# HGRN values of seven heads through memory and VectorE transposes, the residual moved to later jobs, decode rows transposed in one batch, the second group's gate sums later

## The chip, the cores and the metric

The kernel runs on one core of a Trainium2 chip, in one launch. The core has a matrix engine (TensorE, PE in the profile), a vector engine (VectorE, DVE), an activation engine (ScalarE, ACT), a general engine (GpSimd, POOL), and a queue from which DMAs are issued in order (SyncE, SP). Each engine works through its own instructions in order and waits on the others by semaphores. The metric is device time in microseconds (us); the median of three runs before the change is 1764.88 us (1764.72 to 1768.95).

## The reference

One inference step of one decoder layer, in fp32, for a prompt of 1024 tokens and 8 decode rows, 1032 columns in all, with a model width of 1024:

```python
h = rmsnorm(x, w['norm1_w'])
proj = h @ w['w_in']
q_r, f_r, i_r, g_r, z, xbc_r, dt_r = jnp.split(proj, splits, axis=-1)
# group A: HGRN2, 8 heads of 128
f = lb + (1.0 - lb) * jax.nn.sigmoid(f_r)
log_f, k, q = jnp.log(f), 1.0 - f, jax.nn.silu(q_r)
o_a, S_h_new = hgrn2_mix(heads(q), heads(k), heads(i_r), heads(log_f), S_h)
o_a = rmsnorm(o_a, w['hgrn_norm_w']) * jax.nn.silu(heads(g_r))
# group B: Mamba-2, 16 heads of 64 in 2 groups
...
y = y.reshape(Bsz, L, D_SSM) * jax.nn.silu(z)
y = rmsnorm(y.reshape(Bsz, L, SSM_GROUPS, -1), w['ssm_norm_w'].reshape(SSM_GROUPS, -1))
x = x + jnp.concatenate([o_a, y], axis=-1) @ w['w_out']
h = rmsnorm(x, w['norm2_w'])
gate, val = jnp.split(h @ w['w_up'], 2, axis=-1)
gate, buf_f_new = causal_dwconv(gate, buf_f, w['ffn_conv_w'], w['ffn_conv_b'])
x = x + (jax.nn.silu(gate) * val) @ w['w_down']
```

In HGRN2 a head has queries q, keys k, values v (`i_r`) and a forget factor f per key channel. Within a chunk the output is a causal product of q and k with the decays between them, times v; between chunks a state of 128 x 128 is carried. The decode rows each have their own state, which is multiplied by f, gets k times v added, and is read by q. Outputs are the final rows and all new states.

## The kernel before, in words

Tensors stand with channels on the 128 partitions and tokens along the free axis. A product of fp32 precision is made of three passes in a shorter format, high x high, high x low, low x high; every weight tile is therefore loaded (`ws`, line 189), cast by ScalarE to its high half (`wh`, line 190), and VectorE makes the low half (`wl`, line 192). These tiles have two buffers each, and a weight load is issued two jobs ahead. `fetch` (lines 172 to 175) issues other loads on SP, in order behind the last weight load.

PE's order is written out by hand; that of the other engines comes from a planner. The input projection is a list of jobs of 72 matmuls (three chunks of 344 columns, 24 each). For each HGRN head h there are four jobs, f, q, v and sg. `drive` takes a stream of other PE work, cuts it into pieces with weights (the numbers that the stream yields), and places job matmuls between them. While head h is in work, the jobs of head h+1 run; under the last head, head 7, the first jobs of the output projection run. `after(n, work)` runs `work` when n more job matmuls have passed, `spread` runs a row of pieces n matmuls apart.

`head(h, t)`, from line 830, is one such stream. In order: the 8 decode values are transposed (line 834) and eight PE transposes of 128 x 128 turn the head's values v (channels x tokens) into `vt` (tokens x channels) in two PSUM banks, `vtp` (line 839), which ScalarE copies out (line 840). VectorE copies the decode values (line 842), they go to memory (843) and come back spread over the partitions (`vb`). GpSimd multiplies them by k (line 852) and adds them to the states `Sh` (854), which SP stores (855). Then the causal product within a chunk is built in levels: `near` computes small blocks on PE (names `a0` to `a6` in the profile, tile `a`), and between the levels `scale(lv)` multiplies q and k by running products of f: two VectorE products (lines 872 and 873), and, at every other level, two ScalarE copies (875 and 876). The tiles f, k, v and q themselves are the working space: after line 901, which writes q times f into the place of v, they hold scaled keys and queries by turns. `level` picks blocks into `amc` (line 897). At the end come the decode outputs (`od`, copied at line 943), the transposed keys (`ktp`, line 950), the products of keys with values (`kv`, 962 and 964) and the outputs (`o`, 987), where `vt` is first used. `hr_d` and `mix_d` carry the head's result through memory to the output projection.

The gate of the Mamba-2 part (`ssm_gate`, for g of 0 and 1) sums squares over four jobs of z; after the last, for each of three chunks, `rstd` makes a product with ones (`ms`) and three VectorE products (lines 649 to 651), 36 + 14 g matmuls after that chunk's end. After the third chunk `tail` makes four VectorE products of 128 x 1032 (line 694) with four stores. For g = 1 this falls into head 0.

The output projection is a list of jobs (r0.m: four rows of 128 input channels, two blocks of 128 outputs). Jobs 8.0, 8.2, 12.0, 12.2 come first, then 8.4, 8.6, 12.4, 12.6, then those of rows 0 and 4. Their inputs come from memory as `ml`, and are cast to `mh` by ScalarE (line 1023) and split by VectorE (1024). Jobs with r0 = 8 copy PSUM to `x` by ScalarE (line 1064), the others add by VectorE (1066). There are three PSUM banks for these products. The residual is x itself in channel order. At an earlier time 32 DMAs (`token_blocks`, 770 to 776) write x_prompt to memory in blocks of 32 x 32; for each output block, two loads of 128 x 512 (`xs`), two VectorE transposes of 32 x 32 blocks (line 793), and adds on GpSimd (line 790) put it onto `x`. The decode rows are loaded as 8 x 128 (`xd`), transposed on PE (`xtd`, line 797), and added by VectorE (798). This is spread into the jobs with r0 = 8.

Of the kernel before, what the change touches and what calls it, by code (L numbers as in the profile page):

```python
# [16 lines left out]
P = 128  # L17
DM = 1024
T = 1024
# [31 lines left out]
def hybrid_layer(  # L51
# [177 lines left out]
    def after(n, work):  # L229

        later.append([n, work])
# [421 lines left out]
    def ssm_gate(g):  # L653
        acc = []

        def z_job(i):
            j = g * 4 + i

            def begin():
                if i == 0:  # L660
                    acc.append(tl("g", "gacc"))
                if g:
                    ssm_decode(1, i)
                elif i < 2:
                    ssm_decode(0, i + 2)

            def evict(c, cs, ps):
                Y = Xg[g][i][:, cs]
                sz = tl("z", "sz")[:, :CH]
                A.activation(sz, ps, AF.Silu)  # L670
                V.tensor_tensor(Y, Y, sz, op=ALU.mult)
                if i == 0:
                    A.activation(acc[0][:, cs], Y, AF.Square)
                else:
                    A.activation(sz, Y, AF.Square)
                    (V if g or i == 3 else G).tensor_tensor(acc[0][:, cs], acc[0][:, cs], sz, op=ALU.add)
                if i == 3:
                    after(36 + 14 * g, lambda: rstd(c))
            in_job(f"z{j}", OFF_Z + j * P, evict, begin=begin)

        def rstd(c):
            cs = chunks[c]
            ps = bank("ms", "nx")
            mm(ps[:, :CH], ones, acc[0][:, cs])
            rstd_of(acc[0][:, cs], tl("z", "nt")[:, :CH], ps[:, :CH], 512)

            if c == NCH - 1:
                tail()

        def tail():  # L690
            for i in range(4):
                j = g * 4 + i
                Y = Xg[g][i][:, :NT]
                V.scalar_tensor_tensor(Y, Y, col("sn", j), acc[0][:, :NT], op0=ALU.mult, op1=ALU.mult)
                SP.dma_start(mix_d[8 + j], Y)

        for i in range(4):
            z_job(i)
# [29 lines left out]
    def once(work):  # L728
        def run():
# [19 lines left out]
    G.affine_select(eye8, eye8, pattern=[[1, ND], [-1, ND]], compare_op=ALU.is_equal, fill=0.0, base=0,  # L749
                    channel_multiplier=0)  # L750
    vd_d = dram.tile([H, ND, P], F32, name="vd_d")
    hr_d = dram.tile([H, 4, 256], F32, name="hr_d")

    am = const.tile([P, NC, P], F32, name="am")
# [12 lines left out]

    xb_d = dram.tile([KT, P, T], F32, name="xb_d")

    def token_blocks():  # L770
        for m in range(KT):
            for a in range(4):
                f0 = m * P + 32 * a
                SP.dma_start(xb_d[m, 32 * a:32 * a + 32].rearrange("j (b i) -> j b i", i=32),
                             x_prompt[0, :, f0:f0 + 32].rearrange("(b j) i -> j b i", j=32))
                yield

    def residual_load(m):
        ms = slice(m * P, (m + 1) * P)
        xs = [tl("d", "xs")[:, :512] for _ in range(2)]  # L780
        xd = small.tile([ND, P], F32, tag="xd", name=nm("xd"))
        for i in range(2):
            fetch(xs[i], xb_d[m][:, i * 512:(i + 1) * 512])
        fetch(xd, x_sample[:, 0, ms])
        return xs, xd

    def residual(out, xs, xd):

        def add(x_, y_):
            G.tensor_tensor(x_, x_, y_, op=ALU.add)  # L790

        for i0 in range(2):
            V.transpose(xs[i0], xs[i0])
            if i0 == 0:
                add(out[0][:, 0:512], xs[0])
                ps = bank("xtd", "nx")
                PE.transpose(ps[:, :ND], xd, ident[:ND, :ND])
                V.tensor_tensor(out[1][:, 508:516], out[1][:, 508:516], ps[:, :ND], op=ALU.add)
            else:
                add(out[0][:, 512:516], xs[1][:, 0:4])  # L800
                add(out[1][:, 0:508], xs[1][:, 4:512])
            yield
# [3 lines left out]
    def head_in(h):  # L806
        t = {}

        def f_end():
            f, k = t["f"], tl("big", "k")  # L810
            A.activation(f[:, :NT], f[:, :NT], AF.Identity, bias=lbt[:, 0, h:h + 1], scale=lbt[:, 1, h:h + 1])
            V.tensor_scalar(k[:, :NT], f[:, :NT], -1.0, 1.0, op0=ALU.mult, op1=ALU.add)
            t["k"] = k

        for n, off, func in (("f", OFF_F, AF.Sigmoid), ("q", OFF_Q, AF.Silu), ("v", OFF_I, AF.Copy),
                             ("sg", OFF_G, AF.Silu)):
            def evict(c, cs, ps, n=n, func=func):
                A.activation(t[n][:, cs], ps, func)

            def begin(n=n):  # L820
                t[n] = tl("e" if h == 0 and n == "f" else "big", n)

            if h == H - 1 and n == "sg":
                in_job_last(f"{n}{h}", off + h * P, evict, begin)
            else:
                in_job(f"{n}{h}", off + h * P, evict, begin, f_end if n == "f" else None)
        return t

    def head(h, t):
        f, k, q, v, sg = (t[n] for n in ("f", "k", "q", "v", "sg"))  # L830


        dps = bank("vd", "nx")
        PE.transpose(dps[:ND, :P], v[:, T:NT], ident)
        vt = [half("vt"), half("vt")]
        for hf in range(2):
            ps = bank("vtp")
            for i in range(4):
                PE.transpose(ps[:, blk[i]], v[:, hf * 512 + i * P:hf * 512 + (i + 1) * P], ident)
            A.copy(vt[hf], ps)  # L840
# [5 lines left out]
        for b0 in (0, 4):  # L846
            bs = slice(b0, b0 + 4)
            ds = slice(T + b0, T + b0 + 4)
            Sd, vb = tl("ld", "Sh"), tl("d", "vb")[:, :512]
            fetch(d4(Sd), state_hgrn[0, bs, h].rearrange("b k v -> k b v"))  # L850
            fetch(vb, vd_d[h, bs].rearrange("b n -> (b n)").unsqueeze(0).to_broadcast([P, 512]))
            G.tensor_tensor(d4(vb), d4(vb), cb(k[:, ds]), op=ALU.mult)
            V.tensor_tensor(d4(Sd), d4(Sd), cb(f[:, ds]), op=ALU.mult)
            G.tensor_tensor(Sd, Sd, vb, op=ALU.add)
            SP.dma_start(hgrn_sample[0, bs, h].rearrange("b k v -> k b v"), d4(Sd))
            Sds.append(d4(Sd))

# [81 lines left out]
            mm(ops[32 * g:32 * g + 32, :P], qb[:, b, :], Sds[b // 4][:, b % 4, :], start=(b < 4), stop=(b >= 4))  # L941
        odr = small.tile([P, P], F32, tag="odr", bufs=1, name=nm("odr"))
        V.tensor_copy(odr, ops[:, :P])
        yield 3.5

        for hf in range(2):
# [93 lines left out]
    def out_job(r0, m, halves=(0, 1), last=False):  # L1040
        def load():
            w = wload(w_out[0, r0 * P:(r0 + 4) * P, m * P:(m + 2) * P], 4, 2 * P,
                      kept=(r0 // 4 * 4 + m // 2, halves[0]) if len(halves) == 1 else None)
            return w, [residual_load(m + i) for i in range(2)] if r0 == 8 else None

        def run(loads):
            w, res = loads
            if r0 not in mixes:
                mixes[r0] = mix_load(r0)
            hi, lo = mixes[r0]  # L1050
            if res:
                for hf in range(2):
                    xpair[hf][m // 2] = tl("big", "x1")[:, :NT].rearrange("p (i t) -> p i t", i=2)
                    for i in range(2):
                        xh[hf][m + i] = xpair[hf][m // 2][:, i, :]
            for i in range(2):
                for hf in halves:
                    for c in range(2):
                        cs, ts_ = slice(c * QW, (c + 1) * QW), slice((2 * hf + c) * QW, (2 * hf + c + 1) * QW)
                        ps = psmm.tile([P, 512], F32, tag="mm", name=nm("mm"))[:, :QW]  # L1060
                        yield from steps(w, i * P, (i + 1) * P, hi, lo, ts_, ps)
                        x_ = xh[hf][m + i][:, cs]
                        if res:
                            A.copy(x_, ps)  # L1064
                        else:
                            V.tensor_tensor(x_, x_, ps, op=ALU.add)
                        if last:
                            final(m + i, x_, ts_)
                            if hf and c:
                                after(28, lambda m=m + i: weigh(m))  # L1070
                        yield True
                if res:
                    spread(residual([xh[hf][m + i] for hf in range(2)], *res[i]), 8)
        job(f"o{r0}.{m}" + (f".{halves[0]}" if len(halves) == 1 else ""), load, run)

    def final(m, x_, ts_):
# [27 lines left out]
    heads[0] = head_in(0)  # L1104
    ssm_gate(1)
    heads[1] = head_in(1)
    job("conv", None, once(lambda: spread(conv_states(), 60, lambda: spread(token_blocks(), 40))))
    for h in range(2, H):
        heads[h] = head_in(h)

# [395 lines left out]
```

## Time and profile before

| what | value |
|---|---|
| median of 3 runs | 1764.88 us |
| profiled execution | 1763.89 us |
| its span | 1762.2 us, mean TensorE clock 0.994 |
| PE busy | 1713.2 us, 97% |
| VectorE, ScalarE, GpSimd busy | 63%, 46%, 27% |
| head 0 | 380 to 443 us: PE busy 58.3 of 63 |
| head 4 | 631 to 694 us: PE busy 63.0 of 63 |
| head 7 and the output jobs after it | 819 to 930 us: PE busy 101.2 of 111 |
| values: PE transposes `vtp` | 64 x 272 ns; ScalarE copies 16 x 590 ns |
| residual: VectorE transposes `xs` | 16 x 696 ns |

The span runs from the first to the last instruction of the profiled execution; the time of that execution is 1.7 us longer, by what lies around the span. Busy time of PE is modelled from starts and includes overlap, so an entry of 0.32 us can follow the one before by 0.16. "Idle before" and the lists of waits tell what released an engine after a gap. The granted clock is given as a share of full TensorE speed.

### The profile page before, as it was taken

The numbers are of one execution on the slowest core, as the hardware profiler recorded it, in microseconds if no ns is written. First come the engines' busy times: TensorE is split into PE (matmuls) and PEld (weight loads), VectorE is DVE, ScalarE is ACT, GpSimd is POOL, SyncE is SP. The second block draws the span as 40 slices with busy tenths as digits, with TensorE's granted clock in tenths as the row PEclk, the third lists the DMA queues.
The fourth block names the chain that finished last, engine by engine and source line by source line (L and its number), as shares of the span: only waits on it lengthen the run. The fifth ranks groups of instructions, "written<-read, shape, count | busy, mean of one in ns | idle before, by whom it ended". The sixth has DMA issues, their size and how long they took to land. (4 is left out here: it accounts for less than half of the span.)

```text
span 1762.2 us, 38558 instructions
## 1 busy us (share of the span) xinstructions
PE 1713.2 (97%) x16111; PEld 1662.8 (94%) x16111; DVE 1105.4 (63%) x1988; ACT 812.3 (46%) x1450; POOL 482.0 (27%) x485
## 2 busy tenths in 40 slices
PE   7999899999999999999899999999999999999998
PEld 6999799998999999999799989999999999999997
DVE  6668966575554554466636688776667777445545
ACT  7577698454544454454423374334333434111114
POOL 2103332120110110112220355666666664000002
PEclk9999999999999999999899999999999999999999
DMA  5355744643321332234336742222222226422312
GB/s 166 68 147 155 189 117 136 179 139 105 88 89 51 98 87 80 69 115 143 110 113 212 245 127 73 73 85 85 85 73 73 80 78 217 152 85 78 98 61 97
DMA packets 249828, 199.17 MB, mean 113 GB/s; under 512 B 47212, under 2 KB 220822, under 8 KB 249638
## 3 DMA queue, kind: packets, MB, share of 16 engines
q1 hardware_dynamic: 249366, 196.61, 36.8%
q8 instruction: 126, 2.06, 0.5%
q14 instruction: 48, 0.39, 0.1%
q0 software_dynamic: 288, 0.10, 0.0%
HBM read 154.11 MB, written 46.94 MB: 114 GB/s over the span
## 5 line engine op out<-in xcount | busy, mean ns | idle before, releaser
L93 PE MATMUL mm<-hh,wh 128*128 128x344 f32 x1248 | 405.9, 326 | 2.0 <-issue 1.2
L93 PE MATMUL mm<-hl,wh 128*128 128x344 f32 x1248 | 405.5, 325 | 0.0
L93 PE MATMUL mm<-hh,wl 128*128 128x344 f32 x1248 | 402.4, 323 | 0.0
L93 PEld LDWEIGHTS mm<-hh,wh 128*128 128x128 f32 x1248 | 235.4, 189 | 6.5 <-issue 3.9
L93 PEld LDWEIGHTS mm<-hl,wh 128*128 128x128 f32 x1248 | 235.4, 189 | 4.5 <-issue 3.3
L93 PEld LDWEIGHTS mm<-hh,wl 128*128 128x128 f32 x1248 | 235.7, 189 | 1.8 <-issue 1.4
L190 ACT CAST wh<-ws 128x1024 fp32r<-128x1024 f32 x96 | 100.6, 1047 | 254.1 <-PE dn L93 135.0
L93 PE MATMUL ub<-uh,wh 128*128 128x258 f32 x704 | 199.3, 283 | 3.1 <-DVE fext L1319 2.7
L93 PE MATMUL ub<-ul,wh 128*128 128x258 f32 x704 | 199.0, 283 | 0.0
L93 PE MATMUL ub<-uh,wl 128*128 128x258 f32 x704 | 198.7, 282 | 0.0
L93 PE MATMUL dn<-ah,wh 128*128 128x256 f32 (+1 forms) x640 | 181.1, 283 | 2.0 <-DVE x L1436 2.0
L93 PE MATMUL dn<-al,wh 128*128 128x256 f32 (+1 forms) x640 | 180.6, 282 | 0.0
L93 PE MATMUL dn<-ah,wl 128*128 128x256 f32 (+1 forms) x640 | 180.1, 281 | 0.0
L192 DVE TENSOR_TENSOR wl<-ws,wh 128x1024 fp32r<-128x1024 f32 x88 | 108.7, 1235 | 75.7 <-ACT wh L190 68.6
L93 PE MATMUL mm<-mh,wh 128*128 128x258 f32 x512 | 148.2, 289 | 4.1 <-ACT x L1064 2.8
L93 PE MATMUL ua<-uh,wh 128*128 128x258 f32 x528 | 149.6, 283 | 1.3 <-DVE val L1331 1.3
L93 PE MATMUL ua<-ul,wh 128*128 128x258 f32 x528 | 149.3, 283 | 0.0
L93 PE MATMUL ua<-uh,wl 128*128 128x258 f32 x528 | 148.4, 281 | 0.0
L93 PE MATMUL mm<-ml,wh 128*128 128x258 f32 x512 | 146.9, 287 | 0.8 <-DVE ml L1024 0.8
L93 PE MATMUL mm<-mh,wl 128*128 128x258 f32 x512 | 146.5, 286 | 0.0
L93 PEld LDWEIGHTS ub<-uh,wh 128*128 128x128 f32 x704 | 132.9, 189 | 3.8 <-DVE fext L1319 2.9
L1269 DVE TENSOR_TENSOR wl<-wt,wh 128x512 fp32r<-128x512 f32 x88 | 89.6, 1037 | 74.2 <-ACT wh L1268 73.9
(351 smaller groups left out, 4037.2 us busy)
## 6 DMA issues: line engine op xcount, KB each, us to landing
ws<-in_w_in_dram SPq DMA_DIRECT2D x52, 512.0 KB
ws<-in_w_up_dram SPq DMA_DIRECT2D x44, 512.0 KB
ws<-in_w_out_dram SPq DMA_DIRECT2D x24, 512.0 KB
act_d<-val SPq DMA_DIRECT2D x22, 516.0 KB
al<-act_d SPq DMA_DIRECT2D x22, 516.0 KB
ws<-in_w_down_dram SPq DMA_DIRECT2D x22, 512.0 KB
ml<-mix_d SPq DMA_DIRECT2D x48, 172.0 KB
csb<-cs_d SPq DMA_DIRECT2D x32, 256.0 KB
```

Source lines behind the costliest of these rows:

```text
L93: PE.matmul(out, lhsT, rhs, start=start, stop=stop)
L190: A.copy(wh[:, :n], ws[:, :n])
L192: V.tensor_tensor(wl[:, :n], ws[:, :n], wh[:, :n].bitcast(F32), op=ALU.subtract)
L1269: V.tensor_tensor(lo[:, cs], sums[name], hi[:, cs].bitcast(F32), op=ALU.subtract)
```

## The change

It has four parts.

1. In heads 0 to 6 the eight PE transposes and two ScalarE copies of v are gone. When a head's v job has ended, four DMAs write v to memory (`vb_d`) with its 32 x 32 blocks in transposed places, in runs of 32 numbers. 60 matmuls into the head, two loads bring it back as `vt` (128 x 512 each, contiguous by partition), and two VectorE transposes of 32 x 32 blocks, written in the program behind the copy `odr`, finish it in place. Head 7 keeps its PE transposes.
2. The gate sums of g = 1 run 100 matmuls after their chunk in place of 50.
3. The 8 decode rows of x are loaded once as two tiles of 8 x 512, transposed by eight PE transposes into one bank and copied by VectorE to `xsT`, with the first block of `token_blocks`; these pieces are 30 matmuls apart in place of 40. The residual adds `xsT` on GpSimd.
4. The residual of output blocks 0 to 7 runs in the jobs 8.4, 8.6, 12.4 and 12.6, a pair each, in place of 8.0, 8.2, 8.4 and 8.6.

```diff
-                    after(36 + 14 * g, lambda: rstd(c))
+                    after(36 + 64 * g, lambda: rstd(c))
...
+    vb_d = dram.tile([H - 1, P, NC, P], F32, name="vb_d")
...
+    xsT = const.tile([P, KT, ND], F32, name="xsT")
+
     def token_blocks():
+        xs = [half("xd"), half("xd")]
+        for i in range(2):
+            fetch(xs[i][:ND], x_sample[:, 0, i * 512:(i + 1) * 512])
         for m in range(KT):
...
+            if m == 0:
+                ps = bank("xtd", "nx")
+                for k in range(KT):
+                    PE.transpose(ps[:, k * ND:(k + 1) * ND], xs[k // 4][:ND, blk[k % 4]], ident[:ND, :ND])
+                V.tensor_copy(xsT, ps[:, :KT * ND].rearrange("p (k b) -> p k b", b=ND))
 
     def residual_load(m):
-        ms = slice(m * P, (m + 1) * P)
         xs = [tl("d", "xs")[:, :512] for _ in range(2)]
-        xd = small.tile([ND, P], F32, tag="xd", name=nm("xd"))
         for i in range(2):
             fetch(xs[i], xb_d[m][:, i * 512:(i + 1) * 512])
-        fetch(xd, x_sample[:, 0, ms])
-        return xs, xd
-
-    def residual(out, xs, xd):
+        return xs
+
+    def residual(m, xs):
+        out = [xh[hf][m] for hf in range(2)]
...
             if i0 == 0:
                 add(out[0][:, 0:512], xs[0])
-                ps = bank("xtd", "nx")
-                PE.transpose(ps[:, :ND], xd, ident[:ND, :ND])
-                V.tensor_tensor(out[1][:, 508:516], out[1][:, 508:516], ps[:, :ND], op=ALU.add)
+                add(out[1][:, 508:516], xsT[:, m, :])
...
+        def v_end():
+            for b in range(4):
+                SP.dma_start(vb_d[h, :, :, 32 * b:32 * b + 32].rearrange("(a j) c r -> j c a r", j=32),
+                             t["v"][32 * b:32 * b + 32, :T].rearrange("j (c a r) -> j c a r", a=4, r=32))
+
+        ends = {"f": f_end, "v": v_end if h < H - 1 else None}
...
-                in_job(f"{n}{h}", off + h * P, evict, begin, f_end if n == "f" else None)
+                in_job(f"{n}{h}", off + h * P, evict, begin, ends.get(n))
...
+        later_vt = []
         dps = bank("vd", "nx")
         PE.transpose(dps[:ND, :P], v[:, T:NT], ident)
         vt = [half("vt"), half("vt")]
         for hf in range(2):
+            if h < H - 1:
+                later_vt.append((vt[hf], vb_d[h, :, 4 * hf:4 * hf + 4, :]))
+                continue
             ps = bank("vtp")
...
+        def fetch_values():
+            for dst, src in later_vt:
+                fetch(dst.rearrange("p (c n) -> p c n", n=P), src)
+
+        after(60, fetch_values)
...
         V.tensor_copy(odr, ops[:, :P])
+        if h < H - 1:
+            for hf in range(2):
+                V.transpose(vt[hf], vt[hf])
         yield 3.5
...
-            return w, [residual_load(m + i) for i in range(2)] if r0 == 8 else None
+            rm = {(8, 4): 0, (8, 6): 2, (12, 4): 4, (12, 6): 6}.get((r0, m))
+            return w, [(rm + i, residual_load(rm + i)) for i in range(2)] if rm is not None else []
...
-            if res:
+            if r0 == 8:
...
-                        if res:
+                        if r0 == 8:
                             A.copy(x_, ps)
...
-                    spread(residual([xh[hf][m + i] for hf in range(2)], *res[i]), 8)
+                    spread(residual(*res[i]), 8)
...
-    job("conv", None, once(lambda: spread(conv_states(), 60, lambda: spread(token_blocks(), 40))))
+    job("conv", None, once(lambda: spread(conv_states(), 60, lambda: spread(token_blocks(), 30))))
```

## The prediction, made before the changed kernel was run

> **What bounds the kernel now.** I read the page's engine table and its chain first, then the list of TensorE's waits, then the table of windows over the two places that the waits point to, and last the timelines of the instructions that the change moves.
>
> ```profile
> PE 1713.2 (97%) x16111; PEld 1662.8 (94%) x16111; DVE 1105.4 (63%) x1988; ACT 812.3 (46%) x1450; POOL 482.0 (27%) x485
> PE a L93 <- DVE q L873: 2.8, 1, 2.8
> PE mm L93 <- ACT x L1064: 2.8, 1, 2.8
> PE xtd L797 <- DVE odr L943: 2.6, 1, 2.6
> PE a L93 <- issue: 1.9, 1, 1.9
> PE odp L93 <- DVE x L798: 1.5, 1, 1.5
> PE ms L93 <- DVE vd L842: 1.4, 1, 1.4
> PE mm L93 <- DVE ml L1024: 0.8, 1, 0.8
> PE a L93 <- DVE v L873: 0.7, 2, 0.5
> ```
>
> TensorE (PE) is busy 1713.2 of 1762.2 us and is the bound: a change gains only by taking PE work away, by closing a PE gap, or by sparing clock; VectorE (63%), ScalarE and GpSimd have room on average but not everywhere. The waits name the gaps near the change: in head 0 `ms` 1.4 and `a` 2.8 (plus 0.45 of the 0.7 at `a <- v`); in head 7 and the first output jobs 0.8, 2.8, 1.9, 2.6, 1.5 and 0.2, together 9.8 us.
>
> The table of windows (start:end, length, PE busy with its count, PEld, DVE, ACT, POOL, granted PE clock, DMA share, GB/s):
>
> ```profile
> 411.09:414.51 3.42, 3.42 (x65) 3.38 (x49) 2.85 (x5) 1.58 (x3) 0.00 (x0) 0.50 0.17 50
> 631.00:694.00 63.00, 63.00 (x829) 60.99 (x828) 32.16 (x61) 30.53 (x48) 5.58 (x4) 1.00 0.27 78
> 819.00:930.00 111.00, 101.19 (x1188) 97.90 (x1187) 65.04 (x122) 40.50 (x88) 30.56 (x28) 0.95 0.42 130
> 844.59:848.00 3.41, 3.41 (x18) 3.41 (x17) 3.41 (x7) 1.96 (x6) 0.00 (x0) 0.50 0.95 271
> 848.00:854.83 6.83, 4.72 (x84) 4.21 (x83) 6.83 (x13) 5.24 (x14) 3.32 (x3) 1.00 0.32 102
> 854.83:861.65 6.82, 6.36 (x29) 6.34 (x30) 1.17 (x4) 0.75 (x2) 0.14 (x1) 0.50 0.12 39
> 930.00:1000.00 70.00, 70.00 (x583) 69.89 (x582) 41.03 (x83) 25.58 (x44) 12.14 (x15) 1.00 0.71 228
> 1052.00:1060.00 8.00, 4.88 (x36) 4.25 (x36) 7.01 (x12) 5.83 (x11) 2.26 (x2) 1.00 0.00 0
> ```
>
> A gap costs twice. After the idle stretch of head 0, the next 3.42 us run at clock 0.50; after those of head 7, 3.41 and 6.82 us do. Work at 0.50 takes double, so 1.7 us are lost in head 0 and (3.41 + 6.82)/2 = 5.1 in head 7. Head 4 (631 to 694) has no gap at all: there only PE's own work counts.
>
> **The change, part by part.**
>
> *1. The values of seven heads.* Removed are 56 PE transposes and 14 ScalarE copies. What eight transposes cost, from PE's timeline in head 4 (start, length):
>
> ```profile
> 635.95 0.32 PE L93 MATMUL mm<-hh,wl 128*128 128x344 f32 x1
> ...
> 636.21 1.03 PE L839 MATMUL vtp<-ident,v 128*128 128x128 f32 x8
> ...
> 637.24 0.32 PE L93 MATMUL mm<-hl,wh 128*128 128x344 f32 x1
> 637.40 0.32 PE L93 MATMUL mm<-hh,wl 128*128 128x344 f32 x1
> ```
>
> Projection matmuls start 0.16 us apart. The third after 635.95 would start at 636.42; it starts at 637.40. Of these 0.98 us a ninth belongs to the transpose `vd`, which stays: 0.87 per head, 7 x 0.87 = **-6.1 us**. The ScalarE copies go beside PE work and count nothing.
>
> Added are, per head, four SP stores with 128-byte runs, two SP loads and two VectorE transposes. In the changed order of instructions the transposes stand ahead of the second and third scaling (L872, L873) whose results PE's last level products need, and VectorE works in order: a late load holds them up. In heads 1, 4, 5 and 6 the second load stands in SP's queue behind both stores of the decode state (L855), which wait for GpSimd. Head 4 before:
>
> ```profile
> 638.92 1.04 SPq L175 DMA_DIRECT2D vb<-vd_d x2
> ...
> 646.92 3.20 SPq L855 DMA_DIRECT2D out_dram<-Sh x2
> ```
> ```profile
> 643.98 1.22 POOL L852 TENSOR_TENSOR vb<-vb,k 128x512 f32<-128x512 f32 x1 [54.84 <-DMA vb<-vd_d]
> ...
> 648.42 1.29 POOL L854 TENSOR_TENSOR Sh<-Sh,vb 128x512 f32<-128x512 f32 x1
> ```
> ```profile
> 637.23 1.23 DVE L192 TENSOR_TENSOR wl<-ws,wh 128x1024 fp32r<-128x1024 f32 x1 [0.54 <-ACT wh L190]
> ...
> 650.10 0.69 DVE L872 TENSOR_TENSOR f<-f,tt 128x512 f32<-128x512 f32 x1 [0.28 <-PE a L93]
> 650.71 0.68 DVE L873 TENSOR_TENSOR q<-q,tt 128x512 f32<-128x512 f32 x1
> ```
> ```profile
> 652.47 0.61 ACT L876 COPY v<-q 128x512 f32<-128x512 f32 x1
> ```
> ```profile
> 656.44 0.76 PE L93 MATMUL a<-q,f 128*32 128x32 f32 x64
> 657.05 0.69 PE L93 MATMUL a<-v,k 128*16 128x16 f32 x64
> ```
> ```profile
> 862.82 0.32 SPq L175 DMA_DIRECT2D xs<-xb_d  x1
> ```
> ```profile
> 865.86 0.71 DVE L793 STREAM_TRANSPOSE xs<-xs 128x512 f32<-128x512 f32 x1 [8.63 <-DMA xs<-xb_d]
> ```
>
> The `vb` loads go out at 638.92; GpSimd starts 5.06 later and is done at 649.71, 5.73 after that. The changed order puts `wl` behind L901, which fills the 0.54 us that VectorE idles ahead of `wl`; the weight load that waits for `wl`, and `vb` behind it in SP's queue, go some 0.56 later. So the second state store leaves at about 650.3 and `vt1` at about 650.75. A load of that size from such a buffer takes 865.86 - 862.82 = 3.0 us to its transpose, so the transpose runs at 653.75 and the scaling starts at 654.4 to 654.9 in place of 650.10: 4.25 to 4.75 later. Its slack: `q` is ready at 651.39 and PE comes for it at 656.44, 0.88 earlier without the transposes: 4.17. The copy `v` is ready at 653.08 and wanted at 657.05 - 0.88: 3.09. The second decides: 1.2 to 1.7 us, I take 1.4, four times = **+5.6**. Heads 2 and 3 issue `vt1` early enough (head 3 ahead of both state stores, head 2 with `vb` sent directly behind the sums' store) and lose nothing. Each new stall can cost clock as the old ones did. The gaps that did were 1.9 us and more; 1.4 lies below, and I charge **+1** for all four.
>
> [...]
>
> The stores' price in themselves is bounded by the same pattern, already in the kernel:
>
> ```profile
> 30.08 3.52 SPq L774 DMA_DIRECT2D xb_d<-in_x_prompt_dram  x4
> ```
>
> Four stores of 128-byte runs hold SP for 3.5 us. In these heads SP's next urgent entry is a weight load, sent two jobs ahead (a job is 72 x 0.16 = 11 us), the place that they read is overwritten (L901) a job after the last chunk, and they are wanted back 60 matmuls later: 0 us, with up to 3.5 per head if that cover were gone. [...]
>
> *2. Gate sums of g=1, from 50 to 100 matmuls (head 0).* PE no longer meets `ms` behind the transposes (1.4). The four products of the tail move from ahead of scaling 2 to ahead of scaling 3:
>
> ```profile
> 401.65 4.90 DVE L694 SCALAR_TENSOR_TENSOR xbc<-xbc,vcol,gacc 128x1032 f32<-128x1032 f32 x4
> ```
>
> Before, head 0 lost 1.4 + 2.8 + 0.45 + 1.7 of clock = 6.4 us. After, 4.9 us still lie in VectorE's way, with two transposes more (2 x 0.65) and a `vt1` that comes behind both state stores: up to one such gap and its slow stretch remain, 4.9 us by my estimate between 2 and 8. **-1.5**, from -4.5 to +1.5.
>
> *3 and 4. Decode rows, and the residual two to four jobs later.* Eight transposes of 8 rows go into one bank in head 3 or 4 (eight at 0.11 = 0.9 at worst, against eight now: 0). Eight VectorE adds of 0.15 go to GpSimd, which is 27% busy. What moves matters more. Head 7 before, on VectorE and GpSimd:
>
> ```profile
> 833.02 3.31 DVE L1024 TENSOR_TENSOR ml<-ml,mh 128x344 fp32r<-128x344 f32 x3 [1.59 <-ACT mh L1023]
> ...
> 838.53 0.68 DVE L872 TENSOR_TENSOR k<-f,tt 128x512 f32<-128x512 f32 x1
> 839.13 1.77 DVE L873 TENSOR_TENSOR v<-q,tt 128x512 f32<-128x512 f32 x1
> ```
> ```profile
> 839.06 1.91 POOL L790 TENSOR_TENSOR x<-x,xs 128x512 f32<-128x512 f32 x2 [1.60 <-ACT x L1064]
> ```
>
> Three splits `ml` stand ahead of scaling 2 (one after the change), and a scaling that takes 0.68 alone took 1.77 beside the residual adds on GpSimd. `xtd` waits 2.6 for its bank, `odp` 1.5 for a VectorE add behind it: both go with the instruction. Of 9.8 us of gaps I leave 2.5, with no slow stretch, and some 0.4 for transposes that still lie among the splits: 9.8 + 5.1 - 2.9 = **-12**, from -15 (all gone) to -6 (the clock loss is left).
>
> The residual then runs among jobs 8.4 to 12.6, where 930 to 1000 has no gap and VectorE is 59% busy. Its transposes wait for loads of 3.0 us in front of the adds that free PSUM banks. PE has three banks and fills one in 12 matmuls of 0.12 us (583 in those 70 us), 1.4: a wait of 3 us is just covered. **+1**, 0 to 4. The 2.7 us gap at 1055 stands in the last window of the table and cost no clock there. Everything ahead of it shifts by some 10 us, so its place on the 3.41 us grid is open: **+1.2** expected, of 0 or 1.7 and more.
>
> Sum: -6.1 + 5.6 + 1 - 1.5 - 12 + 1 + 1.2 = -10.8. The profiled execution took 1763.89 us (span 1762.2), 1.0 below the median of 1764.88; on the median the sum gives **1754.0**.
>
> **Rivals.**
>
> *A, the values come in time.* If GpSimd finishes 1.4 us sooner, or the planner's first `vt` load carries the scaling, the +6.6 fall away: -17.4, 1747.5. For it: the excess over the slack is only 1.2 to 1.7. Against: `vt1` is issued behind a wait in four heads. Chance 0.25.
>
> *B, slower: the values come late.* If the load is sent or lands over 4 us later than I put it (SP held by a wait of an entry ahead, or the store of 128-byte runs not yet finished), each of the four heads idles 5.4 us and pays 1.7 of clock: +4 x (4 + 1.7) = 23, 1777. It overturns the gain from 10.8/4 = 2.7 us a head on. For it: all four stand behind SP's stores, and a slow stretch follows idle times of 2 us. Against: the loads of the residual, same form, landed in 3.0. Chance 0.14.
>
> *C, the gaps of head 7 only move.* VectorE's residual transposes wait for loads ahead of adds that free banks, and give back what head 7 gains: -10.8 + 12 = +1.2, 1766, no change. For it: VectorE is busy through the next jobs. Against: 59% leaves 29 us in 70, and the transposes add up to 11. Chance 0.13.
>
> *D, only idle time is won.* The stretches at 0.50 stay, after other gaps, and none is added: -10.8 + 5.1 + 1.7 - 1 - 1.2 = -6.2, 1758.7. For it: a grid of 3.41 us and gaps of 1 to 3 us leave it to their phase. Against: 4.72 of 6.83 us busy at full clock and then 6.82 at 0.50, right behind the gap that goes. Chance 0.05. [...]
>
> **How the numbers follow.** My sum has 0.43 and stands between A and C. 0.3% (5.3 us) is about what a measurement here can tell from no change. Forecast, A and D are faster (0.73), C is the same (0.13), B slower (0.14). The range takes A's time less a little (1746.5) up to just short of C (1764).
>
> **What would show it.** PE's count falls by 56; `vtp` is left eight times; the only VectorE transposes of 128x512 in heads 0 to 6 wait for `vt<-vb_d`. Right: in heads 1, 4, 5, 6 PE waits 1 to 2 us at `a` for VectorE or ScalarE's copy, not in 2 and 3; 819 to 930 (some us earlier) is busy to over 97% at clock 1.00; no wait of `xtd`, `odp`, `ms`. Wrong: waits of 4 us and stretches at 0.50 in those heads (B), gaps behind L1066 (C), no wait at `a` at all (A).

## The result and the profile after

The changed kernel takes 1769.13 us (median of 20 runs, 1764.16 to 1776.2) against 1765.11 for the kernel before (20 runs): a ratio of 1.0018, 95% interval 1.001 to 1.0025, or 3.2 us more (the two medians lie 4.0 apart). The forecast was 10.8 us less. The profiled execution took 1767.28 us, with a span of 1765.6 against 1762.2.

The page and the list of PE's waits, changed kernel (line numbers behind 770 have moved: L1066 is now L1093, L1064 is L1091, L872 and L873 are L895 and L896):

```profile
PE 1707.2 (97%) x16055; PEld 1655.9 (94%) x16055; DVE 1098.4 (62%) x1995; ACT 801.1 (45%) x1434; POOL 479.9 (27%) x493
PE ms L93 <- DVE nt L649: 8.2, 1, 8.2
PE mm L93 <- DVE x L1093: 4.5, 6, 1.3
PE mm L93 <- ACT x L1091: 3.2, 1, 3.2
PE a L93 <- DVE q L896: 2.6, 3, 1.4
PE mm L93 <- issue: 2.0, 1, 2.0
PE a L93 <- ACT v L899: 1.9, 3, 0.7
PE mm L93 <- ACT q L831: 1.2, 1, 1.2
```

The 56 matmuls are gone, and so are the waits at `xtd` and `odp`. In their place stands one that the prediction had said would go ("no wait of `xtd`, `odp`, `ms`"): 8.2 us at `ms`, and it is no longer for `vd` but for L649. The table of windows, changed kernel:

```profile
204.85:211.68 6.83, 6.12 (x28) 4.31 (x29) 6.50 (x11) 1.58 (x5) 2.36 (x2) 0.50 0.58 159
390.00:446.00 56.00, 46.62 (x584) 43.97 (x583) 31.58 (x58) 26.45 (x42) 4.57 (x4) 0.94 0.39 114
399.41:406.24 6.83, 3.02 (x18) 2.18 (x21) 3.99 (x6) 1.47 (x2) 0.00 (x0) 0.50 0.28 77
640.00:702.00 62.00, 60.43 (x809) 58.21 (x807) 29.73 (x61) 27.88 (x44) 4.62 (x4) 1.00 0.36 98
846.56:849.97 3.41, 3.41 (x137) 3.14 (x136) 3.41 (x8) 3.41 (x9) 0.00 (x0) 0.50 0.65 235
915.00:970.00 55.00, 51.60 (x423) 50.58 (x422) 38.23 (x68) 18.78 (x34) 12.51 (x16) 1.00 0.66 212
```

Head 0 (from 390) has 9.4 us of gaps and a stretch at half clock; head 4 (from 640), full before, has 1.6 us of gaps; the jobs that now carry the residual (from 915) have 3.4. How the 8.2 us come about is read from four timelines of head 0 of the changed kernel, those of SP, GpSimd, VectorE and PE:

```profile
396.06 0.39 SPq L872 DMA_DIRECT2D out_dram<-Sh  x1
396.49 0.51 SPq L175 DMA_DIRECT2D vt<-vb_d  x1
398.40 0.39 SPq L872 DMA_DIRECT2D out_dram<-Sh  x1
398.89 0.45 SPq L175 DMA_DIRECT2D vt<-vb_d  x1
```
```profile
394.76 1.27 POOL L871 TENSOR_TENSOR Sh<-Sh,vb 128x512 f32<-128x512 f32 x1
...
397.11 1.26 POOL L871 TENSOR_TENSOR Sh<-Sh,vb 128x512 f32<-128x512 f32 x1
```
```profile
392.02 0.69 DVE L896 TENSOR_TENSOR q<-v,tt 128x512 f32<-128x512 f32 x1
399.75 0.71 DVE L969 STREAM_TRANSPOSE vt<-vt 128x512 f32<-128x512 f32 x1 [7.04 <-DMA vt<-vb_d]
402.05 0.71 DVE L969 STREAM_TRANSPOSE vt<-vt 128x512 f32<-128x512 f32 x1 [1.60 <-DMA vt<-vb_d]
402.69 0.48 DVE L649 SCALAR_TENSOR_TENSOR nt<-ms,gacc 128x344 f32<-128x344 f32 x1
```
```profile
403.22 1.51 PE L93 MATMUL ms<-gacc,ones 128*128 128x344 f32 x2 [8.21 <-DVE nt L649]
```

GpSimd ends an addition at 396.03, and only then SP can send the first state store; behind it stands the first load of the values. The second pair goes the same way at 398.4. VectorE stands idle for 7.0 and 1.6 us at the two transposes. L649, the first product on the first chunk's sums, is behind them; it reads the only bank of its PSUM pool, and PE, which wants that bank for the second chunk's `ms`, stops from 395.0 to 403.2.

Head 4 of the changed kernel, SP and VectorE:

```profile
651.51 2.76 SPq L872 DMA_DIRECT2D out_dram<-Sh  x2
654.32 0.97 SPq L175 DMA_DIRECT2D vt<-vb_d  x1
```
```profile
658.05 0.71 DVE L969 STREAM_TRANSPOSE vt<-vt 128x512 f32<-128x512 f32 x1 [5.31 <-DMA vt<-vb_d]
```

Here the second load leaves behind both state stores, as the prediction had it. Its transpose starts 3.7 us later (the prediction took 3.0), the last scaling stands behind it, and PE waits 0.85 and 0.72 us at `a`.

### The profile page after: what moved, and what is told of

The parts are those of the page before. It is cut to its first block, busy times and chain, and to the rows that moved or that the text cites. A ratio compares the mean times of both kernels' runs of the same rounds, so it can differ in the third digit from the quotient of the medians.

```text
span 1765.6 us, 38509 instructions
## 1 busy us (share of the span) xinstructions
PE 1707.2 (97%) x16055; PEld 1655.9 (94%) x16055; DVE 1098.4 (62%) x1995; ACT 801.1 (45%) x1434; POOL 479.9 (27%) x493
## 3 DMA queue, kind: packets, MB, share of 16 engines
q8 instruction: 126, 2.06, 0.5%
```

## The experiments

All times are given against the kernel before, run beside each experiment on the same chip, as the ratio of their runs times 1765 us; the intervals are 0.12 to 0.2% to either side, 2 to 4 us. A difference between two of these kernels carries the intervals of both, so a few us between them are not resolved by the times alone; where the text then goes by gaps, these are those of one profiled execution of each.

**Values asked for earlier**

```diff
-        after(60, fetch_values)
+        after(20, fetch_values)
```

> The loads of the values are asked for 20 matmuls into the head in place of 60, so that SP issues both ahead of the two state stores that wait for GpSimd. Theory (the values come late because their second load stands behind those stores): the 8.2 us wait of PE at ms in head 0 and its stretch at half clock (3.4 us lost) go, and so do the waits at a in heads 1, 4, 5 and 6 (about 7 us): some 18 to 19 us less than the changed kernel, about 15 us less than the kernel before. Rival (VectorE has too much to do in head 0, whenever the values land): heads 1, 4, 5, 6 gain their 7 us, head 0 keeps its loss: about 4 us less than the kernel before.

Measured: 1756.2 us, ratio 0.9956 (0.994 to 0.9972), 7.8 us less than before and 11 less than the changed kernel: about half of the gain expected over the kernel before. Head 0 is cured, which the rival excluded; its waits at `ms` sum to 1.0. Heads 1, 3, 4, 5, 6 still wait, 5.3 us in all, for a new reason. VectorE and GpSimd, this kernel, head 5:

```profile
698.64 0.69 DVE L895 TENSOR_TENSOR k<-k,f 128x512 f32<-128x512 f32 x1
699.25 1.53 DVE L896 TENSOR_TENSOR v<-v,f 128x512 f32<-128x512 f32 x1
...
703.59 1.75 DVE L896 TENSOR_TENSOR q<-v,tt 128x512 f32<-128x512 f32 x1
```
```profile
698.87 1.35 POOL L869 TENSOR_TENSOR vb<-vb,k 128x512 f32<-128x512 f32 x1 [53.65 <-DMA vb<-vd_d]
```

GpSimd's products, four in a row from 698.87 on, now run beside VectorE's scaling, and the scaling takes 1.5 to 1.75 in place of 0.69. In the changed kernel GpSimd began in this head at 710.65, just as the second scaling ended. The earlier loads have changed the order on SP (one load of the values now stands ahead of the loads `vb`); that this is what moved GpSimd's start is not shown.

**State stores sent later**

```diff
-            SP.dma_start(hgrn_sample[0, bs, h].rearrange("b k v -> k b v"), d4(Sd))
+            after(90, lambda bs=bs, Sd=Sd: SP.dma_start(hgrn_sample[0, bs, h].rearrange("b k v -> k b v"), d4(Sd)))
```

> Only the state stores are asked for later (90 matmuls after the GpSimd adds in the program's order). In heads 1 to 6 both loads of the values then go ahead of both stores; in head 0 one store is still ahead of them. Order of VectorE as in the changed kernel. Theory: the waits at a in heads 1, 4, 5, 6 go (about 7 us), in head 0 the second load leaves 2 us earlier and the wait at ms shrinks from 8.2 to some 6.5: 8 to 9 us less than the changed kernel, 4 to 5 less than the kernel before. Rival (the waits at a come from VectorE's two transposes, 1.3 us more work, and not from the load): heads 1, 4, 5, 6 keep at least half of their waits, 2 to 4 us less than the changed kernel.

Measured: 1758.89 us, ratio 0.9964 (0.9949 to 0.9978), 6.4 us less than before, 9.6 less than the changed kernel. Head 4 of this kernel, on SP, on VectorE, and in the windows:

```profile
642.90 1.54 SPq L175 DMA_DIRECT2D vt<-vb_d  x2
648.14 2.76 SPq L872 DMA_DIRECT2D out_dram<-Sh  x2
```
```profile
649.73 1.38 DVE L969 STREAM_TRANSPOSE vt<-vt 128x512 f32<-128x512 f32 x2 [4.49 <-DMA vt<-vb_d]
```
```profile
636.00:698.00 62.00, 62.00 (x820) 59.92 (x820) 31.29 (x63) 29.57 (x46) 4.62 (x4) 1.00 0.36 99
```

SP begins with both loads 5 us ahead of the stores, and PE has no gap, with the same two transposes in the same place on VectorE: the lateness of the load made the waits at `a`, not the VectorE work. VectorE still idles 4.49 us in front of them, which here costs PE nothing. In head 0, where one store is still in front, `ms` waits 7.0, as expected there.

**Values back on PE, the rest of the change kept**

```diff
-        ends = {"f": f_end, "v": v_end if h < H - 1 else None}
+        ends = {"f": f_end, "v": None}
...
-            if h < H - 1:
+            if False:
                 later_vt.append((vt[hf], vb_d[h, :, 4 * hf:4 * hf + 4, :]))
...
-        if h < H - 1:
-            for hf in range(2):
-                V.transpose(vt[hf], vt[hf])
```

> The first part of the change is undone (values transposed on PE as before, no detour through memory), the later gate sums and both parts on the residual stay. Theory (the detour costs more than it gives): no wait at ms, none at a in heads 1 to 6, PE has 6.1 us more work: some 12 to 13 us less than the changed kernel, 8 to 9 less than the kernel before. Rival (the later gate sums themselves hold PE in head 0, by their single bank): head 0 keeps a loss of 8 us and more, and the time is that of the kernel before within 2 us.

Measured: 1756.01 us, ratio 0.995 (0.9937 to 0.9963), 8.8 us less than before, as the theory has it and not the rival. Parts 2 to 4 are a gain; part 1 takes it back.

**Sums in the pool of four banks**

```diff
-            ps = bank("ms", "nx")
+            ps = bank("ms", "mx" if g else "nx")
```

> The sums product ms of the second group writes to the pool of four banks in place of the single bank; nothing else is changed. Theory (PE waits 8.2 us at ms because the first chunk's VectorE products, which free the single bank, stand in VectorE's queue behind the two transposes of late values): the wait at ms goes, PE is held later by the scaling behind the same transposes for 2 us or less: 6 to 10 us less than the changed kernel, about 4 less than the kernel before. Rival (PE waits for the data of the sums, not for the bank): the wait stays and nothing changes.

Measured: 1767.48 us, ratio 1.0015 (1.0003 to 1.0026): 0.5 us less than the changed kernel, no difference that the runs resolve. PE's waits in this kernel:

```profile
PE a L93 <- DVE q L896: 3.5, 4, 2.0
PE ms L93 <- DVE nt L649: 3.2, 2, 2.9
PE mm L93 <- ACT q L831: 2.6, 1, 2.6
```

The second chunk's `ms` no longer waits, so the single bank set where PE stopped; the third chunk's now waits 2.9. The late values hold VectorE all the same: it idles 6.8 and 1.9 us in front of the two transposes. PE then waits 2.6 at a bank copy of ScalarE in place of 1.2. By its gaps and clock, head 0 still loses 7.7 us in place of 10.9. The total does not show these 3 us: in the profiled execution the waits at `a` grow, and 6.8 us near the start run at half clock. My 6 to 10 us were wrong.

**Head 7's stores later**

```diff
-            SP.dma_start(hgrn_sample[0, bs, h].rearrange("b k v -> k b v"), d4(Sd))
+            def put(bs=bs, Sd=Sd):
+                SP.dma_start(hgrn_sample[0, bs, h].rearrange("b k v -> k b v"), d4(Sd))
+            n_put = 200 if h == H - 1 else 0
+            if n_put:
+                after(n_put, put)
+            else:
+                put()
```

> On the changed kernel, only head 7 sends its two state stores later: three loads of ml go ahead of the first store and three ahead of the second, in place of all twelve behind both. Theory (the 3.2 us wait of PE for the bank copy at L1091 in head 7 comes from ScalarE standing at a cast of ml whose load is held in SP's queue behind the stores that wait for GpSimd): that wait shrinks to under 1 us and its stretch at half clock (1.7 us) goes: 4 to 5 us less than the changed kernel, so about the time of the kernel before. Rival (the residual work or VectorE's splits hold it): the wait stays and the time is that of the changed kernel.

Measured: 1768.25 us, ratio 1.0016 (1.0002 to 1.0029), 0.4 us less than the changed kernel, where 4 to 5 were expected. SP of the changed kernel, and SP of this one:

```profile
837.27 3.19 SPq L872 DMA_DIRECT2D out_dram<-Sh  x2
840.56 5.72 SPq L175 DMA_DIRECT2D ml<-mix_d  x12
```
```profile
832.61 1.62 SPq L175 DMA_DIRECT2D ml<-mix_d  x3
835.32 0.39 SPq L873 DMA_DIRECT2D out_dram<-Sh  x1
```

The wait at the bank copy fell from 3.24 to 1.46 us, not under 1, and the stretch at half clock behind it is gone. So the loads behind the stores made a good half of that wait. The total did not show it: in the profile of this run head 0 waits 8.7 at `ms` with 10.2 us at half clock, and 6.8 us at half clock follow the gap at 1054 where 3.4 did. A gain of 3 us in one place does not stand out of such shifts.

**Later gate sums alone, on the kernel before**

```diff
-                    after(36 + 14 * g, lambda: rstd(c))
+                    after(36 + 64 * g, lambda: rstd(c))
```

> The kernel before with the second part of the change alone: gate sums of the second group 100 matmuls after their chunk in place of 50. Theory (part 2 is a gain by itself: it clears head 0, and only together with late values does it hold PE at ms): head 0 loses 2 us or less in place of 6.4, 4 to 5 us less than the kernel before. Rival (the later sums cost by themselves): no gain, or slower.

Measured: 1760.24 us, ratio 0.997 (0.9958 to 0.9981), 5.3 us less. Part 2 alone is a gain of the size expected.

**Residual back in its first jobs, on the changed kernel**

```diff
-            rm = {(8, 4): 0, (8, 6): 2, (12, 4): 4, (12, 6): 6}.get((r0, m))
+            rm = m if r0 == 8 else None
```

> The changed kernel with its fourth part undone: the residual of blocks 0 to 7 runs in jobs 8.0, 8.2, 8.4 and 8.6 again (decode rows still come from the batch). Theory (moving the residual takes waits out of head 7 and gives most of them back behind the adds of the later jobs, 3.4 us at L1093): the waits at L1093 between 920 and 960 us go, head 7 and the jobs after it get 3 to 8 us of waits and slow stretches more: 0 to 4 us slower than the changed kernel. Rival (the residual in the later jobs is a loss by itself): 3 us less than the changed kernel.

Measured: 1768.25 us, ratio 1.001 (0.9998 to 1.0022), 1.4 us less than the changed kernel and not distinct from it. The windows of this kernel:

```profile
829.00:915.00 86.00, 79.83 (x940) 77.78 (x941) 54.52 (x95) 31.02 (x68) 31.65 (x34) 1.00 0.43 130
915.00:970.00 55.00, 54.67 (x457) 54.46 (x456) 35.15 (x69) 21.25 (x37) 3.99 (x4) 1.00 0.68 220
```

Its later jobs lose 0.3 us in place of 3.4, and head 7 loses 6.2 in place of the changed kernel's 4.3 and 1.7 of clock: 6.5 in place of 9.4. The waits at L1093 in these jobs all but went, as the theory has it, and others came in head 7, but the balance of the two places, some 3 us less, is the rival's. The total decides between neither. A later experiment on another kernel points the other way.

**Loads of head 0 early and stores late together**

```diff
-        after(60, fetch_values)
+        after(60 if h else 20, fetch_values)
...
+            n_put = 200 if h == H - 1 else 90
```

(the rest of `put` as above)

> The changed kernel with the values asked for 20 matmuls into head 0 (60 in the others) and the state stores sent later in all heads, so that neither the loads of the values nor those of ml stand behind a store that waits for GpSimd. Theory: head 0 loses 2 to 3 us in place of 12.8, heads 1 to 6 under 1 in place of 7, head 7 about 2 in place of 6: 18 to 22 us less than the changed kernel, 14 to 18 less than the kernel before. Rival (part of the gain is lost to new waits of PE elsewhere, as in the run with all values early): 9 to 12 less than the kernel before, as the best of the first four runs.

Measured: 1747.97 us, ratio 0.9896 (0.9881 to 0.9912), 18.4 us less than before, 21.5 less than the changed kernel: at the upper end of what was expected, and better than both kernels. (The 12.8 us that the expectation gives head 0 count the whole length of its stretches at half clock; by the work done in them it is 10.9.) Its windows for head 0, head 7, and the jobs with the residual; head 4 is full:

```profile
390.00:446.00 56.00, 54.31 (x644) 51.40 (x643) 36.73 (x67) 31.61 (x48) 5.93 (x4) 1.00 0.39 113
809.00:895.00 86.00, 83.58 (x1090) 81.47 (x1089) 53.98 (x101) 35.10 (x77) 19.44 (x20) 1.00 0.45 139
895.00:950.00 55.00, 52.49 (x434) 51.86 (x433) 37.80 (x69) 19.07 (x34) 12.34 (x16) 1.00 0.66 213
```

**The same with the values on PE** (the edit of the third experiment on the kernel above)

> The kernel with late stores and early loads, but with the values transposed on PE as before (first part of the change undone). Theory (the first part gives its 6.1 us of PE work once the loads are not held up): 5 to 7 us slower than the kernel with late stores and early loads, so 10.5 to 12.5 less than the kernel before. Rival (the detour brings nothing net, VectorE and SP take back what PE gives): within 2 us of the kernel with late stores and early loads.

Measured: 1754.02 us, ratio 0.9927 (0.9912 to 0.9942): 5.5 us slower than with the detour, as the theory has it, with some 4 us to either side, since the two kernels ran at different times. Once its loads are not held up, part 1 gives about what its PE work costs.

**The first part alone, on the kernel before** (`vb_d`, `v_end`, `later_vt`, `fetch_values` at 60 and the two VectorE transposes as in the change, nothing else)

> The kernel before with the first part of the change alone. VectorE's order in head 0: the transposes, then the third chunk's sums, the four products of the tail, then the scaling. Theory: heads 1, 4, 5, 6 lose 7 us, seven heads win 6.1, head 0 loses 10 to 13 in place of 6.4 because the values' loads stand behind both stores and the tail behind the transposes: 4 to 8 us slower than the kernel before. Rival (head 0 suffers only with the later gate sums): within 2 us of the kernel before.

Measured: 1779.17 us, ratio 1.0068 (1.0048 to 1.0089), 12.0 us slower: the direction of the theory, and more than its 4 to 8. PE's waits:

```profile
PE a L93 <- DVE q L890: 5.5, 5, 2.1
PE xtd L798 <- DVE odr L960: 4.5, 1, 4.5
PE ms L93 <- DVE vd L853: 4.3, 1, 4.3
```

Besides the waits at `a`, PE now reaches the first `ms` 0.87 us sooner and waits 4.3 for its bank, which `vd` still holds. The PE transposes of values had stood just there and covered part of that wait; before, it was 1.4. The copy of `vd` that frees the bank comes late: just ahead of it VectorE idles 2.2 us at a product of the decode state (`Sh` times f) that waits for its load. In head 7 the wait at `xtd` has grown from 2.6 to 4.5. Added to the third experiment, +12.0 for part 1 and -8.8 for the others make +3.2, the measured change; with the intervals of both that holds within some 4 us.

**The best kernel with the residual in its first jobs** (the edit of the residual experiment on it)

> The kernel with late stores and early loads, with the residual back in jobs 8.0, 8.2, 8.4 and 8.6. Theory (moving the residual only moves its waits): within 3 us of the kernel with late stores and early loads, with the waits at L1099 gone and new ones in head 7. Rival (the later place is worth the 10 us that head 7 lost before the change): 6 us and more slower than the kernel with late stores and early loads.

Measured: 1750.66 us, ratio 0.991 (0.9894 to 0.9926), 2.5 us slower than the best kernel, within the theory's 3 us, though some 4 us to either side do not quite rule out the rival's 6. The wait at the bank copy in head 7 is 3.35 us although the stores are late: three splits `ml` take 3.36 us beside GpSimd there, as they took 3.31 in the kernel before. So the place of the residual is worth something in this kernel and, by the gaps, the reverse in the changed kernel; its sign is not settled.

## Why the prediction was wrong, by its steps

- *56 transposes, -6.1.* Borne out: PE's busy time fell by 6.0 us, and the best kernel with and without the detour differs by 5.5, give or take 4.
- *Heads 1, 4, 5, 6, +5.6 and +1 of clock.* Right in cause and place, and nearly in size. The gaps at `a` are 0.39 and 0.67 (head 1), 0.85 and 0.72, 0.34 and 0.41, 1.35 and 0.72: 5.45 us, none in heads 2 and 3. No stretch at half clock followed, so the +1 did not come. A further 2.0 us in head 5 are put down to issue, which I had not foreseen. They are gone in the kernel with late stores, so they seem to belong to the late loads; what PE waits for there the trace does not show.
- *Head 0, -1.5.* This is the step that failed most. Its text has "up to one such gap and its slow stretch remain, 4.9 us by my estimate between 2 and 8", and that PE no longer meets `ms`. Measured: 8.21 + 1.16 of gaps, and 1.5 of clock (3.02 us of work at 0.50), 10.9, against 6.4 before: +4.5, 6 us off and beyond the step's range. The late load was in the step. I followed who waits for the scaling behind the late transposes, and not who waits for the sums' own products behind them: they stand in VectorE's queue too, and free a pool of one bank. Parts 2 and 1 were summed one by one, but part 2 moved those products behind what part 1 delays. Alone, part 2 gave 5.3 us. In head 0, by gaps and clock, part 1 costs 3.6 us on the kernel before (10.0 against 6.4) and 10 with the other parts (10.9 against 0.8 in the third experiment). In the totals this interplay does not show: part 1 costs 12.0 us either way, since alone it loses more elsewhere.
- *Head 7, -12.* The waits at `xtd` and `odp` went. But 1.04 + 3.24 and 1.7 of clock are left, 6.0 in place of 2.9: a gain of 8.7, within the range of the step. The crowding of VectorE and GpSimd that the step saw (a scaling of 1.77 us in place of 0.68) was there before, but another wait took its place. ScalarE stands before PE's bank copy in both kernels, before (first) and after the change (second):

```profile
838.09 0.62 ACT L875 COPY k<-f 128x512 f32<-128x512 f32 x1 [1.84 <-DVE f L872]
```
```profile
843.60 1.40 ACT L1049 CAST mh<-ml 128x344 fp32r<-128x344 f32 x3 [5.94 <-DMA ml<-mix_d]
```

Before, it waits for VectorE's scaling; after, for a load of `ml`. All twelve loads of this group now leave behind both state stores (from 840.56 on), where four left ahead of the first store before. It is the very pattern that I had priced for `vt`, and the fifth experiment bears it out for a good half of the wait.

- *Later jobs, +1.* Waits at L1093 grew from 1.2 to 4.5, and one of 0.8 at the next product: some +4, the end of the step's range. The row that I leant on (59% busy, a wait of 3 us just covered) is an average.
- *The gap at 1055, +1.2.* For the most part (2.35 of 2.72 us) it fell into one window of the 3.41 us grid: 3.4 us at half clock, 1.5 lost. That was a matter of phase, and the forecast said so.
- Not in the sum: the gap at 202, untouched by the change, is followed by 6.83 us at half clock where 3.42 were (6.12 and 3.42 us of work), 1.35 lost by phase.

Of the rivals, B's mechanism (loads held behind a wait on SP) was also the forecast's own; the 4 us more that B gave each of four heads did not come there, and the price came in head 0. C came in part: head 7 gained 8.7 us and the later jobs gave back 4.1, not all of it. That the measured time lies near C's 1766 is chance, since more than half of what parts it from the forecast is not C's. I let the rivals exclude each other; parts of both came, on top of the forecast's own stalls. Added with what the profile shows (-6.1 + 5.45 + 2.0 + 4.5 - 8.7 + 4.1 + 1.5 + 1.35, with head 7 from 14.7 to 6.0), the steps give +4.1, against +3.4 between the two spans.

## What to carry to other kernels

In head 0 of the changed kernel the second state store left SP at 398.40, after GpSimd's addition that ends at 398.37, and the second load of the values behind it at 398.89; PE stood for 8.21 us. So for every load that a change adds, ask what stands ahead of it in its queue, and send stores that nobody waits for after loads that somebody does. Here that order on SP alone (stores later, head 0's loads earlier) turned 3.2 us lost into 18.4 gained. Where a change puts a waiting instruction into an engine's order, list everything queued behind it, small products that free a single PSUM bank first of all (here L649, behind two transposes that waited 7.04 and 1.60 us), and price the parts of a change together where they meet on one queue, as in head 0.

## What the runs showed of the hardware

**Half clock and idle time, as these profiles show them.** The stretches at 0.50 start on a grid of 3.413 us in the profiles before and after (before: 206.29, 411.09, 844.59, 854.83; after: 204.85, 399.41, 846.56, 1058.19). PE's idle time in each window of that grid, apart from the first 15 and the last 10 us: at full clock, the windows followed by one at 0.50 had 2.06, 2.42, 1.90 and 2.10 us of idle time (before) and 2.42, 3.41, 3.12 and 2.34 (after); no other had more than 1.70 (before) and 1.57 (after). At half clock, the next window stayed at 0.50 after 0.47 us of idle time (before), 0.71 and 3.41 (after), and was at full clock after 0.40 and 0.38 (after) and after none (both). One stretch does not fit: in the kernel with the sums in the pool of four banks, 40.5 to 47.3 us ran at 0.50 with no idle time in it or in the window ahead of it; its cause is open. So here the same gap cost by its phase: the one of 2.72 us at 1055 of the kernel before is in two windows, with 1.30 and 1.70 us of idle time, and costs no clock; in the changed kernel 2.34 us of idle time are in one window, and 3.41 us at half clock follow. Two kernels with a gap of some 3 us before the same bank copy in head 7, state stores late (first) and values early (second):

```profile
830.61:834.02 3.41, 1.89 (x16) 1.69 (x15) 1.09 (x3) 1.31 (x3) 0.00 (x0) 1.00 0.86 248
834.02:837.43 3.41, 2.34 (x136) 2.18 (x136) 3.41 (x9) 3.41 (x9) 0.00 (x0) 1.00 0.98 330
```
```profile
829.61:833.02 3.41, 1.12 (x10) 0.91 (x8) 1.23 (x3) 1.38 (x4) 0.00 (x0) 1.00 0.94 283
833.02:839.84 6.82, 5.90 (x147) 5.63 (x148) 6.82 (x14) 5.91 (x15) 0.00 (x0) 0.50 0.62 202
```

The first (2.59 us) is split by a grid line, 1.52 and 1.07, and costs no clock (the next window is at 1.00 as well); the second (3.21) leaves 1.12 us busy in one window, and 5.90 us of work run at 0.50. At 0.50 the projection's matmuls start 0.287 us apart (412 to 414 us of the kernel before) in place of 0.158, which is 1.8 times and not double: a full stretch of 3.41 us loses 1.5 us, and the 1.7 of the prediction and of the sums above are a tenth too large.

**VectorE beside GpSimd.** In the first experiment a VectorE product of two tiles of 128x512 took 0.69 us alone, and three took 1.53, 1.52 and 1.75 beside GpSimd's products: 0.8 to 1.1 us more for each. In head 7 of the kernel before it was 0.68 (at 838.53) and 1.77 (at 839.13, beside the residual adds). Not every one that overlaps GpSimd's work is longer: the one at 826.25 of that kernel took 0.69.
